# A one-layer hybrid decoder step: gate and rotary arithmetic moved into PSUM, loads and gate parts reordered

## Chip, cores and metric

One core of one Trainium2 chip runs one launch of the kernel. The metric is the device time of that launch in microseconds (us).

## What is computed

One layer with two branches, for a prompt of 1024 tokens and 8 decode sequences of 8 new tokens over 4096 cached tokens each (1088 tokens in all, width 1024, everything float32). The reference, cut:

```python
def hybrid_layer(x, pos, ssm_h0, attend, w):
    xn = rmsnorm(x, w["norm_in"])
    u_s, g_s, cq, ckv_raw, kr_raw, g_a, m_s, m_a = split_in(xn @ w["w_in"])
    y_s, h_last = s5_branch(u_s, ssm_h0, w)      # scan, gelu -> zg, then
    #   zg * sigmoid(zg @ ssm_w_glu + ssm_b_glu)    (the gated unit, "GLU")
    y_s = (y_s * silu(g_s)) @ w["w_br_ssm"]
    cq = rmsnorm(cq, w["mla_q_norm"])                     # 384 wide
    q = einsum('blr,rhd->blhd', cq, w["mla_w_uq"])        # 16 heads, 64 + 32
    q_rope = apply_rope(q[..., 64:], cos, sin)
    q_lat = einsum('blhd,chd->blhc', q[..., :64], w["mla_w_uk"])
    ckv = rmsnorm(ckv_raw, w["mla_kv_norm"])              # 256 wide
    k_rope = apply_rope(kr_raw, cos, sin)
    o_lat = attend(q_lat, q_rope, ckv, k_rope)   # causal over the prompt; decode:
    #   32 pages of 128 rows per sequence, found by page_table, and the own 8
    o = einsum('blhc,chd->blhd', o_lat, w["mla_w_uv"])
    y_a = (o * silu(g_a)) @ w["w_br_attn"]
    merged = sigmoid(m_s) * y_s + sigmoid(m_a) * y_a
    return x + merged @ w["w_out"], ...          # then a final rmsnorm
```

## The kernel before

**Precision and form.** Every product is three matmuls: an operand is split into a rounded high part (a cast on ScalarE, ACT) and the rest (a subtraction on VectorE, DVE, or GpSimd, POOL), and `mm3`/`mm3s` (L141 to L168) multiply high by high, high by low and low by high. `split` (L93 to L102) is the helper: casts stand under L96, subtractions under L102. Activations lie transposed in SBUF, 128 channels by 1088 tokens, which are worked in three pieces of 368, 368 and 352 tokens.

**Gate parts.** A dense product against 128 columns of a weight is a part: a load of 512 KB on SyncE's (SP's) queue (`wraw`), a cast and a subtraction of the weight, 24 matmuls for each of the three token pieces (`mm`), and an end for each token piece: for the gates `g_s` and `g_a`, a tanh on ACT into `gst` (L803) and a DVE operation (L804) that multiplies it with the matmul's bank. Gate parts need only the normalised input, so they serve as filler for TensorE (PE) between stages whose other engines are late. `PLAN` says how many parts lie where.

**Order.** Stages are generators; `woven` interleaves their steps by given weights, and a scheduler puts each engine's instructions in order by recorded priority. Each engine works its own list strictly in that order. `pin` and `behind` tie instructions to others by hand. PSUM's banks are handed out by `bank` in two names, `tr` and `sc`, beside `mm` and `acc`.

**The stages in time** (us from the span's start): the input's norm and transposes to 30; the S5 stages with gate parts to 360; the latents (`stage_latents`, 360 to 465), where `cq` and `ckv` are made by `load_wide`'s 384-wide weights (`wraw` cut in pieces of 128, `wwhi`, `wwlo`), then one `turn` per 128 tokens: norm (`cqn`, L868), transposes on PE (L835). Beside it `cache_ropes` gathers the cached rotary keys (`dkr`) with indirect DMAs from POOL, lays them anew on POOL (`dks`, L1234), transposes them on PE and writes high, high and low parts to `kr_dram`. `cache_rows` (the row indices for these gathers, from the page table) stands just ahead of it. `q_rope` (480 to 518) makes the rotary queries: PE's product into a bank, two copies of swapped halves to `qrot` (ACT), their product with the sine table (POOL L903), the bank times the cosine table into `qr` in SBUF (DVE L904), the sum (L905), the split (`qh`, `ql`). Then the values and other keys and queries, and the prompt's attention (677 to 980), set up by `attn_setup` (transposes of `kst`, splits into the K tiles, the `causal` mask's load) and by `dec_setup` (the new tokens' own rotary keys, `kss` and `krs`). The gated unit (`stage_glu`) and other dense parts are woven with the end of that attention and the decode attention (1130 to 1530; `decode`: per 512 cached rows a gather `ck`, its split into `ch` (ACT) and `cl` (POOL, one operation of 1024), transposes, scores, and products with the values). The dense rest runs to the end.

Of the kernel before, what the change touches and what calls it, by code (L numbers as in the profile page):

```python
# [77 lines left out]
class Body:  # L78
# [51 lines left out]
    def load_wide(self, c0, ncol, raws, outs):  # L130
# [39 lines left out]
    def constants(self):  # L170
# [4 lines left out]
        nc.sync.dma_start(self.ident, a["k_ident"])  # L175
# [4 lines left out]
        self.g_dram = {k: d.tile([D, TOK], F32, name=f"g_{k}") for k in ("gs", "ga", "ms", "ma")}  # L180
        self.gates_done, self.marks, self.first_load, self.x_last, self.banks = {}, [], None, None, 0
# [589 lines left out]
    def s5_states(self, sb, ps):  # L771
# [3 lines left out]
        for r, (c0, n) in enumerate(((0, P), (P, P), (2 * P, NPR))):  # L775
# [9 lines left out]
            nc.sync.dma_start(dst, st[:n])  # L785


    def stage_gates(self, keys, raws, outs, sb, ps, first=0, n=KT, pin=False, goals=None, late=False):
        nc = self.nc
        cols = {"gs": C_GS, "ms": C_MS, "ga": C_GA, "ma": C_MA}  # L790
        for key in keys:
# [21 lines left out]
    def stage_latents(self, lp, cq, outs, sb, ps, between):  # L813
# [71 lines left out]
        yield 4.0  # L885
        turn(*last.pop())


    def q_rope(self, s, qsb, sb, ps, tabs):
# [5 lines left out]
        for t0, m in CHUNKS:  # L895
# [3 lines left out]
            q = sb.tile([P, 368], F32, name="qr", bufs=2)[:, :m]  # L899
            r = sb.tile([P, 368], F32, name="qrot", bufs=2)[:, :m]  # L900
# [3 lines left out]
            nc.vector.tensor_mul(q, b[:, :m], tabs[0][:, t0:t0 + m])  # L904
# [827 lines left out]
    def build(self):  # L1732
# [205 lines left out]
```

## Time and profile before

| | before |
|---|---|
| median of 3 runs | 1761.27 us (1760.45 to 1765.47) |
| the profiled execution | 1759.65 us, its span 1757.8 us |
| PE busy | 1688.1 us (96%) |
| DVE / ACT / POOL busy | 66% / 53% / 34% |
| mean granted clock of PE | 0.987 |

The profile is of one execution. The span runs from its first to its last instruction; 1.85 us of the execution lie outside it. Busy times of the engines overlap. The granted clock is PE's share of its full speed; 0.50 is the lower of its two levels.

### The profile page before, as it was taken

The numbers are of one execution on the slowest core, as the hardware profiler recorded it, in microseconds if no ns is written. First come the engines' busy times: TensorE is split into PE (matmuls) and PEld (weight loads), VectorE is DVE, ScalarE is ACT, GpSimd is POOL, SyncE is SP. The second block draws the span as 40 slices with busy tenths as digits, with TensorE's granted clock in tenths as the row PEclk, the third lists the DMA queues.
The fourth block names the chain that finished last, engine by engine and source line by source line (L and its number), as shares of the span: only waits on it lengthen the run. The fifth ranks groups of instructions, "written<-read, shape, count | busy, mean of one in ns | idle before, by whom it ended". The sixth has DMA issues, their size and how long they took to land.

```text
span 1757.8 us, 31271 instructions
## 1 busy us (share of the span) xinstructions
PE 1688.1 (96%) x10954; PEld 1588.1 (90%) x10954; DVE 1158.4 (66%) x2640; ACT 934.4 (53%) x2226; POOL 592.5 (34%) x622
## 2 busy tenths in 40 slices
PE   6999999989999999999998999999999999999997
PEld 5999999989989998999997898998988999899976
DVE  6768898333374343878888788567656666654496
ACT  5146657722354443767777556456656566631144
POOL 1000000013442204656663555654545445400012
PEclk9999999999999999999999999999999999999999
DMA  8555344544478988665667552575555455384322
GB/s 218 123 144 153 110 120 122 144 139 113 138 222 292 315 299 242 159 167 149 189 162 220 141 158 64 179 251 187 179 172 175 156 170 188 120 303 145 101 85 102
DMA packets 258309, 299.52 MB, mean 170 GB/s; under 512 B 40448, under 2 KB 215272, under 8 KB 251880
## 3 DMA queue, kind: packets, MB, share of 16 engines
q1 hardware_dynamic: 247976, 240.90, 47.7%
q0 software_dynamic: 7872, 48.24, 8.1%
q10 hardware_dynamic: 2304, 8.39, 1.3%
q8 instruction: 87, 1.43, 0.4%
q14 instruction: 70, 0.57, 0.1%
HBM read 201.79 MB, written 95.66 MB: 169 GB/s over the span
## 4 chain that ended last, share of the span: by engine, by line
PE 78%; DMA 8%; DVE 4%; issue 4%; ACT 3%; POOL 2%; SPq 1%; POOLq 0%; ACTq 0%; DVEq 0%
PE mm L159 40%; PE sc L1028 5%; PE sc L159 5%; PE acc L1193 4%; PE tr L1064 3%; PE tr L159 3%; DMA ck<-cache_ckv,pidx 2%; PE acc L1077 2%; PE acc L1078 2%; PE sc L1167 2%; PE sc L1256 1%; PE tr L1256 1%; PE tr L1167 1%; POOL cl L102 1%; DMA wraw<-w_in 1%
## 5 line engine op out<-in xcount | busy, mean ns | idle before, releaser
L159 PE MATMUL mm<-xT,whi 128*128 128x368 f32 (+1 forms) x1920 | 503.9, 336 | 8.7 <-ACT xT L253 4.8
L159 PEld LDWEIGHTS mm<-xT,whi 128*128 128x128 f32 x1920 | 340.9, 190 | 12.6 <-ACT xT L253 5.3
L159 PE MATMUL mm<-xT,wlo 128*128 128x368 f32 (+1 forms) x960 | 320.6, 334 | 0.2 <-DVE wlo L102 0.2
L102 POOL TENSOR_TENSOR cl<-ck,ch 128x1024 fp32r<-128x1024 f32 x64 | 154.2, 2411 | 163.8 <-ACT ch L96 149.4
L159 PEld LDWEIGHTS mm<-xT,wlo 128*128 128x128 f32 x960 | 182.4, 190 | 1.6 <-DVE wlo L102 0.5
L96 ACT CAST pTh<-tr 128x256 fp32r<-128x256 f32 (+1 forms) x248 | 110.8, 449 | 85.9 <-PE tr L1064 67.1
L102 DVE TENSOR_TENSOR pTl<-tr,pTh 128x256 fp32r<-128x256 f32 (+1 forms) x248 | 126.3, 512 | 41.2 <-ACT pTh L96 24.2
L1028 PE MATMUL sc<-K,Q 128*128 128x384 f32 (+5 forms) x576 | 131.5, 345 | 4.0 <-ACT p L1040 4.0
L1045 POOL TENSOR_SCALAR p<-p,sm 128x128 f32<-128x128 f32 (+7 forms) x128 | 96.8, 761 | 109.4 <-DVE sm L1044 48.5
L1040 ACT ACTIVATE p<-sc,sm 128x128 f32<-128x128 f32 (+2 forms) x192 | 110.7, 584 | 22.9 <-DVE sm L1035 12.7
L96 ACT CAST whi<-wraw 128x1024 fp32r<-128x1024 f32 (+1 forms) x76 | 73.3, 966 | 93.1 <-PE mm L159 79.9
L1229 POOL DMA_INDIRECT dkr<-cache_krope,pidx x32 | 33.0, 1032 | 264.2 <-DMA gkv<-mla_kv_norm 256.7
L1064 PE MATMUL tr<-ident,p 128*128 128x128 f32 x576 | 112.1, 274 | 7.6 <-DVE pTl L102 6.7
L159 PE MATMUL mm<-z,whi 128*128 128x368 f32 (+1 forms) x384 | 110.4, 349 | 2.3 <-ACT gst L801 2.3
L1032 DVE TENSOR_REDUCE sm<-sc 128x1 f32<-128x128 f32 (+2 forms) x192 | 104.2, 551 | 9.9 <-PE sc L1028 6.8
L159 PE MATMUL mm<-aT,whi 128*128 128x368 f32 (+1 forms) x384 | 107.6, 337 | 1.6 <-ACT th L1432 1.6
L1028 PEld LDWEIGHTS sc<-K,Q 128*128 128x128 f32 x576 | 98.3, 189 | 11.2 <-ACT p L1040 6.3
L159 PE MATMUL mm<-oT,whi 128*128 128x368 f32 (+1 forms) x384 | 94.2, 327 | 0.2 <-DVE gl L1464 0.2
L102 DVE TENSOR_TENSOR wlo<-wraw,whi 128x1024 fp32r<-128x1024 f32 (+1 forms) x54 | 61.6, 1142 | 39.7 <-ACT whi L96 36.1
L1064 PEld LDWEIGHTS tr<-ident,p 128*128 128x128 f32 x576 | 72.2, 140 | 14.3 <-DVE pTl L102 5.1
L96 ACT CAST ch<-ck 128x1024 fp32r<-128x1024 f32 x64 | 67.3, 1053 | 29.1 <-DMA ck<-cache_ckv,pidx 12.7
L1078 PE MATMUL acc<-pTl,Vt 128*128 128x256 f32 (+1 forms) x224 | 81.6, 364 | 0.1
(534 smaller groups left out, 4390.0 us busy)
## 6 DMA issues: line engine op xcount, KB each, us to landing
wraw<-w_in SPq DMA_DIRECT2D x45, 512.0 KB
krT<-kr_dram SPq DMA_DIRECT2D x64, 192.0 KB
kr_dram<-krx SPq DMA_DIRECT2D x64, 128.0 KB
v_dram<-vt SPq DMA_DIRECT2D x32, 256.0 KB
Q<-qn_dram SPq DMA_DIRECT2D x32, 256.0 KB
K<-kn_dram SPq DMA_DIRECT2D x32, 256.0 KB
Vt<-v_dram SPq DMA_DIRECT2D x8, 1024.0 KB
u_dram<-ust SPq DMA_DIRECT2D x64, 68.0 KB
```

Of the source, the lines that this page charges most:

```text
L96: nc.scalar.copy(hi, src)
L102: return e.tensor_sub(lo, src, hi.bitcast(F32))
L159: i = nc.tensor.matmul(ps, row(s, k)[:, wsl], row(m, k)[(slice(None),) + xsl], start=start and k == j == 0, stop=stop and k == nk - 1 and ...
L1028: self.mark(nc.tensor.matmul(s[:, :w], qq[:, i * P:(i + 1) * P], kk[:, k0:k0 + w], start=j == 0, stop=j == 2), j == 0)
L1032: V.reduce_max(sm[:, x:x + 1], s[:, :w], axis=AX.X)
L1040: nc.scalar.activation(p[:, k0:k0 + w], s[:, :w], AF.Exp, bias=sm[:, 2:3], scale=SCALE, accum_out=sm[:, 3 + x:4 + x])
L1045: nc.gpsimd.tensor_scalar(p[:, :n], p[:, :n], sm[:, 5:6], 0.0, op0=ALU.mult, op1=ALU.add)
L1064: self.mark(nc.tensor.transpose(b[:, x * P:(x + 1) * P], ptl[x][:, k * P:(k + 1) * P], self.ident), x == s0)
L1077: self.mark(nc.tensor.matmul(po[:, o0:], w, th[:, o0:], start=k == 0, stop=False))
L1078: nc.tensor.matmul(po[:, o0:], w, tl[:, o0:], start=False, stop=k == nk - 1)
L1167: i = nc.tensor.matmul(s, x[:, k], y[:, k], start=x is qlh and k == 0, stop=False)
L1193: self.mark(nc.tensor.matmul(o[:, :KV], t[:kp, i * P:(i + 1) * P], pv(i)[x], start=j == 0 and i == 0, stop=j == 2 and i == nt - 1), i == 0)
```

## The change

Seven edits that share a file:

1. `cache_rows` runs behind `stage_x` at the start, not ahead of `cache_ropes`; the loads of `ident` and `norm_in`, and the stores of the S5 states (`sto`), go to ACT's queue.
2. `load_wide` loads its pieces at a higher priority, and `w1`'s casts and subtractions are put behind given gate ends; an unused tile (`gap`) shifts what lies behind it in SBUF.
3. One gate part's first step (`beyond`) is taken ahead of the latents' last `turn`.
4. `cache_ropes` transposes `dkr` itself (no `dks`, no POOL copy) and writes two parts, not three; `dec_keys` gathers `krT` with three loads where there was one.
5. `q_rope` keeps product and sum in the PSUM bank; two gate parts are woven with it instead of one behind one; `own_keys` moves ahead of it out of `dec_setup`.
6. `attn_setup` lays its tiles in another order in SBUF and splits by head, not by half; `PLAN` puts 3 gate parts around the attention's start a little earlier.
7. `stage_glu` applies tanh and the gate in the PSUM bank against `zr`, a row block of z loaded again from DRAM, not against a sum made on POOL (`zz`); `decode` makes `cl` in four POOL operations.

```diff
-PLAN = ((6, MQ, MP - 1), (6, MP - 1, MP - 1), (3, MP + 2, MP + 14), ...
+PLAN = ((6, MQ, MP - 1), (6, MP - 1, MP - 1), (3, MP - 1, MP + 12), ...
...
     def load_wide(self, c0, ncol, raws, outs, behind=None):
...
-            nc.sync.dma_start(raw, self.a["w_in"][:, c0 + s:c0 + s + n].rearrange("(k p) c -> p k c", p=P))
-            self.split(hi[:, :, s:s + n], lo[:, :, s:s + n], raw, "act", "dve")
+            with self.tc.high_priority(offset=UW):
+                nc.sync.dma_start(raw, self.a["w_in"][:, c0 + s:c0 + s + n].rearrange("(k p) c -> p k c", p=P))
+            i = nc.scalar.copy(hi[:, :, s:s + n], raw)
+            j = nc.vector.tensor_sub(lo[:, :, s:s + n], raw, hi[:, :, s:s + n].bitcast(F32))
+            if behind is not None:
+                self.behind(i, behind[0])
+                self.behind(j, behind[1])
...
-        nc.sync.dma_start(self.ident, a["k_ident"])
+        nc.scalar.dma_start(self.ident, a["k_ident"])
...
-            nc.sync.dma_start(dst, st[:n])
+            nc.scalar.dma_start(dst, st[:n])
...
-        w1 = self.load_wide(C_CQ, QL, sb, outs)
+        w1 = self.load_wide(C_CQ, QL, sb, outs, self.gate_ends[-4])
...
         yield 4.0
+        yield next(beyond)
         turn(*last.pop())
...
-            q = sb.tile([P, 368], F32, name="qr", bufs=2)[:, :m]
-            r = sb.tile([P, 368], F32, name="qrot", bufs=2)[:, :m]
+            r = sb.tile([P, 368], F32, name="qrot", bufs=4)[:, :m]
...
-            nc.vector.tensor_mul(q, b[:, :m], tabs[0][:, t0:t0 + m])
+            q = b[:, :m]
+            nc.vector.tensor_mul(q, q, tabs[0][:, t0:t0 + m])
             nc.vector.tensor_add(q, q, r)
...
-        self.KTs = [[kp.tile([P, SEQ], F32R, name=f"K{h}{x}") for x in range(2)] for h in range(2)]
-        self.QTs = [[kp.tile([P, SEQ], F32R, name=f"Q{h}{x}") for x in range(2)] for h in range(2)]
+        for n in ("Q11", "K00", "K01", "causal", "Q00", "Q01", "K10", "K11", "Q10"):
+            t[n] = kp.tile([P, P], F32, name=n) if n == "causal" else kp.tile([P, SEQ], F32R, name=n)
...
-            c = slice(half * 512, half * 512 + 512)
-            for h, rows in ((0, slice(64, 128)), (1, slice(0, 64))):
-                hi, lo = self.KTs[h]
+            banks.append(b)
+        for h, rows in ((0, slice(64, 128)), (1, slice(0, 64))):
+            hi, lo = self.KTs[h]
+            for half, b in enumerate(banks):
...
-            if 0 <= j - 1 < n:
-                ks = kss[j - 1] = sb.tile([P, 2, P], F32, name="dks", bufs=2)
-                nc.gpsimd.tensor_copy(ks.rearrange("p g (r i) -> p g r i", i=4), krs.pop(j - 1).rearrange("p g i r -> p g r i"))
...
-                for y, x in enumerate((hi, hi, lo)):
-                    nc.sync.dma_start(self.kr_dram[j - 2, :, y].rearrange("g p k -> p g k"), x.bitcast(F32))
+                for y, x in enumerate((hi, lo)):
+                    nc.sync.dma_start(self.kr_dram[j - 1, y], x.rearrange("p g k -> p (g k)").bitcast(F32))
...
-        nc.sync.dma_start(krT.bitcast(F32), self.kr_dram[j // 2, j % 2].rearrange("y (r i) k -> (y r) (i k)", i=4))
+        for y in range(3):
+            nc.sync.dma_start(krT[y * NR:(y + 1) * NR].bitcast(F32).rearrange("r (i k) -> r i k", i=4),
+                              self.kr_dram[j // 2, y // 2].rearrange("(i r) (g k) -> g r i k", i=4, g=2)[j % 2])
...
-                self.split(*c, rows(b * 8 + g), "act", "pool")
+                src = rows(b * 8 + g)
+                nc.scalar.copy(c[0], src)
+                for i in range(4):
+                    Gp.tensor_sub(c[1][:, i], src[:, i], c[0][:, i].bitcast(F32))
...
-            nc.gpsimd.tensor_add(zz[:, :m].rearrange("p (c t) -> p c t", t=8), zh.rearrange("p t c -> p c t"),
-                                 zl.rearrange("p t c -> p c t"))
-            nc.vector.scalar_tensor_tensor(g[:, :m], th[:, :m], 1.0, g[:, :m], op0=ALU.add, op1=ALU.mult)
-            nc.vector.tensor_mul(zz[:, :m], zz[:, :m], g[:, :m])
-            nc.sync.dma_start(self.a_dram[rows, sl], zz[:, :m])
+            nc.scalar.activation(b, b, AF.Tanh, scale=0.25, bias=bg[:, j:j + 1])
+            nc.vector.scalar_tensor_tensor(b, b, 1.0, zr[:, :, t0 // 8:(t0 + m) // 8], op0=ALU.add, op1=ALU.mult)
+            g = g[:, :m].rearrange("p (c t) -> p c t", t=8)
+            nc.vector.tensor_mul(g, b.rearrange("p t c -> p c t"), g)
...
+                zrow[j] = sb.tile([P, 8, NCK], F32, name="zr", bufs=1)
+                nc.sync.dma_start(zrow[j], self.z_dram[j * P:(j + 1) * P])
...
-                        yield from self.woven((ropes(), 17), (self.stage_gates(first=6, n=7, **gate), W5))
-                        yield from self.stage_gates(first=7, n=8, pin=True, **gate)
+                        self.own_keys(lp, sb, ps)
+                        yield from self.woven((ropes(), 17), (self.stage_gates(first=6, n=8, **gate), 2 * W5))
```

What this does to the lists of the engines, at three places.

SP's list of transfers between the S5 stages' last stores (`y_dram`) and the latents. L121 is an ordinary part's weight, L137 (L140 in the changed kernel) a piece of `load_wide`'s. Before:

```order
L747 DMA y_dram<-Y 16x8x136 x8
L785 DMA ssm_sample<-sto 128x256 x2
L785 DMA ssm_prompt<-sto 32x256
L1209 DMA sel<-k_sel 8x128
L1211 DMA j_4084<-k_j 128x1
L1213 DMA pt<-page_table 8x32x1
L823 DMA gq<-mla_q_norm 128x384
L824 DMA gkv<-mla_kv_norm 128x256
L826 DMA rt<-k_rope_tok 128x288
L137 DMA wraw<-w_in 128x8x128 x2
L121 DMA wraw<-w_in 128x8x128
L806 DMA g_ga<-gst 128x1088
```

and with the change:

```order
L756 DMA y_dram<-Y 16x8x136 x8
L140 DMA wraw<-w_in 128x8x128 x2
L833 DMA gq<-mla_q_norm 128x384
L834 DMA gkv<-mla_kv_norm 128x256
L838 DMA rt<-k_rope_tok 128x288
L122 DMA wraw<-w_in 128x8x128
L816 DMA g_ga<-gst 128x1088
L140 DMA wraw<-w_in 128x8x128 x3
```

The first two wide pieces stand right behind the last store, ahead of the nine transfers that were before them (six of these have left this place); the third comes behind a gate's store in both.

PE's list at the latents' end: `cqn` 128x128 and 128x64 are the transposes of the last two turns, `mm<-xT` the gate part that follows. Before:

```order
L159 MATMUL mm<-wwhi,xT_7_107 64x288
L835 MATMUL sc<-ident,cqn 128x128 x2
L1239 MATMUL sc<-ident,dks 128x128 x2
L835 MATMUL tr<-ident,cqn 128x64 x2
L159 MATMUL mm<-xT_0_92,whi 128x368
L159 MATMUL mm<-xT_0_93,whi 128x368
```

and with the change, first where the gate part begins and then where it ends:

```order
L166 MATMUL mm<-wwhi,xT_7_107 64x288
L847 MATMUL sc<-ident,cqn 128x128 x2
L1258 MATMUL tr<-ident,dkr 128x128 x2
L166 MATMUL mm<-xT_0_92,whi 128x368
L166 MATMUL mm<-xT_0_93,whi 128x368
```

```order
L166 MATMUL mm<-xT_7_107,whi 128x368
L166 MATMUL mm<-xT_7_106,wlo 128x368
L1258 MATMUL sc<-ident,dkr 128x128 x2
L847 MATMUL tr<-ident,cqn 128x64 x2
L166 MATMUL mm<-xT_0_92,whi 128x368
```

Between the two pieces stand the other matmuls of the same 24, which are now ahead of the last turn's two transposes.

DVE's list at the attention's start: `K` are the key splits, `kss` the own keys, the additions of `causal` the first masks. Before:

```order
L102 TENSOR_TENSOR K_7171<-tr,K_7170 64x512
L102 TENSOR_TENSOR K_7173<-tr,K_7172 64x512
L804 SCALAR_TENSOR_TENSOR gst<-gst,mm 128x368 x2
L1131 CAST kss<-krt 64x32
L1132 COPY kss<-kss 64x32
L1133 COPY kss<-kss 64x32
L1031 TENSOR_TENSOR sc<-sc,causal 128x128 x2
L1134 TENSOR_TENSOR kss<-krt,kss 64x32
L102 TENSOR_TENSOR K_7171<-sc,K_7170 64x512
```

and with the change:

```order
L103 TENSOR_TENSOR K_7104<-sc,K_7103 64x512
L103 TENSOR_TENSOR K_7109<-sc,K_7108 64x512
L813 SCALAR_TENSOR_TENSOR gst<-gst,mm 128x368
L103 TENSOR_TENSOR K_7104<-tr,K_7103 64x512
L1050 TENSOR_TENSOR sc<-sc,causal 128x128 x2
L1051 TENSOR_REDUCE sm<-sc 128x1
L813 SCALAR_TENSOR_TENSOR gst<-gst,mm 128x368
```

`kss` is gone from here, and one K split more stands ahead of the masks; a gate's end now stands behind them.

## Rows read from the trace of the kernel before

**Rows 1.** The page: busy time, share of the span and instructions of each engine.

```profile
PE 1688.1 (96%) x10954; PEld 1588.1 (90%) x10954; DVE 1158.4 (66%) x2640; ACT 934.4 (53%) x2226; POOL 592.5 (34%) x622
```

**Rows 2.** PE's waits in the whole span: waited for, us in total, times, longest.

```profile
PE tr L251 <- DVE xst L199: 8.5, 2, 8.3
PE tr L1064 <- DVE pTl L102: 6.7, 6, 2.1
PE tr L1256 <- DMA ck<-cache_ckv,pidx: 5.7, 4, 2.8
...
PE mm L159 <- DVE gst L804: 3.9, 2, 3.5
PE mm L159 <- ACT wwhi L96: 3.6, 1, 3.6
PE tr L835 <- DVE cqn L868: 3.5, 2, 2.0
...
PE tr L1136 <- DVE kss L1134: 1.8, 1, 1.8
...
PE mm L159 <- DVE wwlo L102: 0.8, 1, 0.8
```

**Rows 3.** Windows: us, busy of PE, PEld, DVE, ACT, POOL, granted clock, DMA.

```profile
373.70:377.10 3.40, 3.14 (x10) 3.14 (x11) 1.78 (x3) 0.26 (x1) 0.00 (x0) 0.50 0.68 191
465.90:469.30 3.40, 3.40 (x13) 3.40 (x12) 0.00 (x0) 0.00 (x0) 1.70 (x2) 0.50 0.44 88
517.10:523.90 6.80, 5.91 (x19) 5.91 (x20) 2.05 (x5) 0.58 (x2) 1.84 (x2) 0.50 0.93 283
687.70:691.10 3.40, 3.40 (x13) 3.27 (x11) 1.75 (x4) 0.97 (x3) 2.98 (x4) 0.50 1.02 296
```

**Rows 4.** SP's queue ahead of the latents: start, us, what.

```profile
349.24 3.02 SPq L785 DMA_DIRECT2D ssm_sample<-sto  x2
...
359.38 1.05 SPq L137 DMA_DIRECT2D wraw<-w_in  x2
```

**Rows 5.** ACT in the same stretch: start, us, what, idle before it and its end.

```profile
371.60 1.04 ACT L96 CAST wwhi<-wraw 128x1024 fp32r<-128x1024 f32 x1 [4.13 <-DMA wraw<-w_in]
```

**Rows 6.** POOL in the latents, by start.

```profile
445.99 0.61 POOL L1234 COPY dks<-dkr 128x256 f32<-128x256 f32 x1 [2.80 <-DMA kr_dram<-dks]
```

**Rows 7.** The rotary queries' stage, one window, columns as in group 3.

```profile
495.00:525.00 30.00, 25.71 (x141) 25.09 (x140) 23.60 (x36) 14.73 (x33) 13.75 (x15) 0.89 0.82 234
```

**Rows 8.** Lines L905 and L904: count, ns least/median/most, first and last start, shapes.

```profile
L905 DVE TENSOR_TENSOR qr<-qr,qrot x12: 512/532/1905, 482.3 to 515.9; 128x368 f32<-128x368 f32 x8, 128x352 f32<-128x352 f32 x4
L904 DVE TENSOR_TENSOR qr<-sc,tab x6: 511/529/542, 481.3 to 511.3; 128x368 f32<-128x368 f32 x4, 128x352 f32<-128x352 f32 x2
```

**Rows 9.** DVE's groups, 478 to 518 and (last two) whole span: busy, mean ns, idle before.

```profile
L102 DVE TENSOR_TENSOR ql<-qr,qh 128x368 fp32r<-128x368 f32 (+1 forms) x12 | 10.8, 902 | 1.1 <-ACT qh L96 0.6
...
L1438 DVE SCALAR_TENSOR_TENSOR gl<-th,gl 128x368 f32<-128x368 f32 (+1 forms) x24 | 23.9, 994 | 9.6 <-ACT th L1432 7.4 <-DMA o_dram<-oT 2.1
L1439 DVE TENSOR_TENSOR zz<-zz,gl 128x368 f32<-128x368 f32 (+1 forms) x24 | 19.9, 829 | 0.5
```

**Rows 10.** DVE at the attention's start.

```profile
684.06 0.50 DVE L1031 TENSOR_TENSOR sc<-sc,causal 128x128 f32<-128x128 f32 x2 [4.43 <-DMA causal<-k_causal]
```

**Rows 11.** POOL's groups in the whole span.

```profile
L102 POOL TENSOR_TENSOR cl<-ck,ch 128x1024 fp32r<-128x1024 f32 x64 | 154.2, 2411 | 163.8 <-ACT ch L96 149.4 <-PE sc L1256 14.2
L1090 POOL TENSOR_TENSOR oT<-oT,og 64x512 f32<-64x512 f32 x32 | 41.5, 1298 | 25.4 <-DVE oT L1083 17.7 <-DMA K<-kn_dram 2.6 <-issue 2.6
L1234 POOL COPY dks<-dkr 128x256 f32<-128x256 f32 x32 | 22.1, 690 | 130.2 <-DMA kr_dram<-dks 103.7 <-DVE wlo L102 7.2 <-DVE qr L904 5.3
```

**Rows 12.** SP's queue at the start.

```profile
0.74 0.40 SPq L175 DMA_DIRECT2D ident<-k_ident  x1
```

**Rows 13.** PE's waits, 676 to 692, and the window of the decode attention.

```profile
PE sc L1028 <- ACT p L1040: 1.8, 1, 1.8
...
1130.00:1540.00 410.00, 398.45 (x2668) 367.64 (x2669) 277.98 (x559) 253.03 (x510) 205.73 (x116) 0.99 0.55 180
```

More of the change, by code (lines that the diff above doesn't have):

```diff
@@ L128, in load_w, with load_wide @@
         return res
-    def load_wide(self, c0, ncol, raws, outs):
+    def load_wide(self, c0, ncol, raws, outs, behind=None):
         nc = self.nc
@@ L981, in attn_setup @@
         nc, a = self.nc, self.a
-        self.causal = kp.tile([P, P], F32, name="causal")
+        t = {}
+        for n in ("Q11", "K00", "K01", "causal", "Q00", "Q01", "K10", "K11", "Q10"):
+            t[n] = kp.tile([P, P], F32, name=n) if n == "causal" else kp.tile([P, SEQ], F32R, name=n)
+        self.causal = t["causal"]
         nc.sync.dma_start(self.causal, a["k_causal"])
-        self.KTs = [[kp.tile([P, SEQ], F32R, name=f"K{h}{x}") for x in range(2)] for h in range(2)]
-        self.QTs = [[kp.tile([P, SEQ], F32R, name=f"Q{h}{x}") for x in range(2)] for h in range(2)]
+        self.KTs, self.QTs = ([[t[f"{n}{h}{x}"] for x in range(2)] for h in range(2)] for n in "KQ")
+        banks = []
         for half in range(2):
@@ L1126, in dec_setup, with own_keys @@
                 nc.sync.dma_start(self.qs[r0:r0 + 16].bitcast(F32), qr[half])
-        kst = sb.tile([NS, P + NR], F32, name="kss", tag="p3", bufs=1)
+    def own_keys(self, lp, sb, ps):
+        nc = self.nc
+        kst = sb.tile([NS, P + NR], F32, name="kss", bufs=1)
         khr = kst[:, P:].bitcast(F32R)
@@ L1136, in dec_setup @@
         nc.tensor.transpose(b[:96, :NS], kst[:, :96], self.ident[:NS, :NS])
[L1137 removed]
+        self.krs = lp.tile([96, NS], F32R, name="krs")
         nc.vector.tensor_copy(self.krs, b[:96, :NS])
@@ L1223, in cache_ropes @@
         nc, a = self.nc, self.a
-        krs, kss = {}, {}
+        krs = {}
         n = DB * 4
-        for j in range(n + 2):
+        for j in range(n + 1):
             if j < n:
@@ L1620, in squares @@
             pt = P if i < 8 else NS
-            y = sb.tile([P, 512], F32, name="osq", bufs=1)
+            y = sb.tile([P, 3, 4, NS], F32, name="osq", tag="oms", bufs=1).rearrange("p a b c -> p (a b c)")[:, 0:512]
             nc.scalar.activation(y[:pt], X[:pt, i, halves[c]], AF.Square, accum_out=ss[:pt, i, c:c + 1])
@@ L1757, in front @@
                         yield from self.stage_x(xT, wr, wo, gsb, self.pool(s3, "xs", 2, side=R), ps)
+                    with ExitStack() as s3:
+                        self.cache_rows(self.pool(s3, "krw", 1, side=R), ps)
                     yield from self.stage_u(wr, wo, gsb, ps, 2, NU)
@@ L1780, in qkv @@
                     outs = self.pool(s2, "wsp2", 1)
+                    more = self.stage_gates(first=5, n=6, pin=True, **gate)
                     yield from self.stage_latents(lp, cq, outs, self.pool(s2, "lsb", 2), ps,
-                                                  self.stage_gates(first=4, n=5, pin=True, **gate))
-                yield from self.stage_gates(first=5, n=6, pin=True, **gate)
+                                                  self.stage_gates(first=4, n=5, pin=True, **gate), more)
+                yield from more
                 with ExitStack() as s2:
```

52 lines of the change are left out of this document (28 added, 24 removed).

## The prediction, made before the changed kernel was run

> **What bounds the kernel now.** The page comes first. TensorE (PE) is busy for 1688.1 us, 96% of the span, and no other engine is above 66% [rows 1]. The change leaves PE's matmul work as it is, so it can only win from the 70 us in which PE stands still and from stretches in which PE works at its lower clock. PE's waits over the whole span say where it stands still [rows 2]: 8.3 us at the start, 3.6 and 0.8 for the wide weights, 3.5 for the latents' norms, 3.5 of 3.9 for a gate's end, 1.8 for the own keys, 6.7 for the attention's low parts, 5.7 for cached rows. No wait is large; the gain is a sum of small ones. The windows of the granted clock add something that this list does not show. [...] PE is the bound there, so work that takes 3.4 us at half speed would take 1.7: each such stretch costs 1.7 us (3.4 for the long one) on top of the wait itself. If the wait goes, I expect the slow stretch behind it to go too.
>
> **The change part by part.** Durations are those of the profiled execution, 1759.65 us, which is 1.62 under the median of the three runs; the sum is made on the first and 1.62 is added at the end.
>
> *Start.* The load of `ident` holds SP's queue for 0.40 us ahead of x's first tiles [rows 12], for which PE waits. On ACT's queue it costs nothing, since ACT has no data yet. The second moved load stands behind x's and counts at most the same for the weights. Gain 0.4 to 0.9; I take 0.5, as the first is sure.
>
> *Wide weights.* SP issues the first two pieces at 359.38 [rows 4]; ACT casts the third of the first set only when it lands, at 371.60, after 4.13 us of idleness [rows 5]. PE waits 4.4 us for the cast and the subtraction, and then works 3.4 us at half clock: 6.1 us. With the change the first two pieces follow the last store directly, without the nine transfers that were ahead of them. The third waits for a buffer that the first frees, so it moves with them. The state stores alone began 10 us ahead of the first piece [rows 4], so a third piece that moves forward by half of this already covers the wait. If the third alone stays late, some 2 us are left to win. Range 2 to 6.1; I take 5.5, nearer to the whole.
>
> *Latents' last turns.* PE waits twice for `cqn`, 3.5 us, the longer 2.0, and then has 3.4 us at half clock [rows 2, 3]. The longer stands in front of the last turn's transposes. Now 24 gate matmuls lie ahead of these transposes. The row at 465.9 counts 13 matmuls in 3.40 us at half clock, so I estimate at least 3.1 us for 24 at full clock, over one and a half times the wait. That gains 2.0 and 1.7. The shorter wait, 1.5 us, has another cause: POOL waits 2.80 us in order for a store before the copy `dks`, and the norm's scale stands behind it on POOL [rows 6]. The copy is removed (32 of them, 22.1 us, 103.7 us of such waiting [rows 11]). But POOL's next gather must now wait until PE has read its buffer, so I count 0.9 of the 1.5. Together 4.6, range 2 to 5.2.
>
> *Rotary queries.* PE waits 3.5 us for a gate's end and then has 6.8 us at half clock, together 6.9. The cause is DVE: in a window of 30 us it is busy for 23.6 [rows 7], and the gate's end stands in its list behind the rotary operations. Some of these are stretched while POOL works. `ql` takes 902 ns in the mean [rows 9] and L905 up to 1905 with a median of 532, whereas L904, which reads a PSUM bank, never goes above 542 [rows 8]. The change moves the operand of L905 and of the split into PSUM, so both should take about 0.53; for `ql` alone that is 12 times 0.37, 4.4 us of DVE time in that stage. Against that, two gate parts lie beside it, whose ends DVE must also make, and the bank is held through the whole chain of operations. I take 5.5 of 6.9; the low end is 2, if DVE stays the bound.
>
> [...]
>
> *Attention's start.* DVE stands idle for 4.43 us until the mask `causal` lands, at 684.06 [rows 10]. The own keys and the second K split are queued behind it, and PE waits 1.8 us for the keys, 1.8 for the first probabilities [rows 13] and has 3.4 us at half clock: 5.3 us. The keys leave this place (they are made 200 us earlier under gate matmuls), and all but one K split stand ahead of the mask. The mask's load still stands behind a load of values on SP's queue. If it lands as late, a gate's end is what then waits behind it, and with it PE's `mm` bank. I take 2.5, about half; ends 0 and 5.3.
>
> *Gated unit.* DVE's two operations of a piece take 994 and 829 ns in the mean [rows 9] beside POOL's sums and would take about 0.53: 24 times 0.76 is 18 us of DVE time. But PE waits for DVE's low parts only 6.7 us there, and part of that comes from other POOL work, which stays. The new loads of `zr` (8 of 0.56 MB, one buffer) can only start when DVE is done with the previous block, and DVE would then wait in order with the softmax behind it; where parts follow one another closely, that costs 1 or 2 us. Range -2 to 6.7; I take 2.5.
>
> *Decode.* `cl` in four operations: from 1298 ns for 512 elements and 2411 for 1024 [rows 11], a line gives 0.745 us for 256 and 2.98 for four, 0.57 more than now per tile. POOL is busy for 206 of 410 us in that window, PE for 398 [rows 13], so the time itself is hidden; but the next gather is issued behind it, and the four waits for `ck` (5.7 us) can grow by 0.57 each. On the other side no DVE operation is held for 2.4 us any more. `krT` has three loads in place of one, issued ahead of their tiles. I take a loss of 1, ends a loss of 3 and a gain of 1.
>
> Everything else (PLAN, `osq`, index loads) I count at nothing: it moves filler and small work under matmuls.
>
> Sum: 0.5 + 5.5 + 4.6 + 5.5 + 2.5 + 2.5 - 1 = 20.1. 1759.65 - 20.1 + 1.62 = 1741. All low ends together give 1.4 (with 0.4 for the start) and 1760, all high ends 32.1 and 1729.
>
> **The rivals.** *Half comes back.* The stages stay tight on DVE, DMA or banks, and the wait moves to the next instruction. For it: the mask is still late, DVE is nearly full beside the rotary queries, and the wide weights' third piece still waits for a buffer. Against it: the last turn's cover is longer than its wait. Taking 2.5 off for the mask, 3.5 for the rotary queries and 3.5 for the weights leaves 10.6 and 1751.
>
> *Nothing is left.* The clock stretches and waits reappear elsewhere, and the new `zr` loads hold DVE in several blocks: about 8 blocks by 1 us, 2 more in decode, from the 10.6 just worked out. That is about 1761. For it speaks only that so many places change at once.
>
> *Slower: the gathers of the decode attention.* If every gather is on the path, `cl`'s 0.57 us is paid in all 64 tiles, 36 us, and the time is 1741 + 35 = 1776, as 1 us of it is in the sum. It decides the sign from some 37 of 64 tiles on (21.1 / 0.57). Four waits for `ck` in the whole span speak against it, as does POOL's half idleness. How far ahead of its tile each of the other 60 gathers lands, I have not worked out; this is why the chance is not smaller.
>
> **How the numbers follow.** The forecast has a chance of 0.58, half of it back 0.22, nothing left 0.11, slower 0.09. About 0.3% (5.3 us) is what a measurement of this kernel can tell from no change. The first two cases are faster than that: 0.80. The third is no change: 0.11. The last is slower: 0.09. For the forecast alone I give 1734 to 1748. The range reaches down to 1733 and up over the second case to 1757, which leaves out the last two and little else, under 2 in 10 with a few of the forecast's own.
>
> **What would show it.** Right: no `wwhi`, `cqn` or `kss` among PE's larger waits; granted clock near 1.0 at 360 to 380, 455 to 475, 495 to 525; the sums in PSUM at 0.51 to 0.54 us each; POOL without L1234 and L1436. Wrong: a wait on `gst` behind the rotary queries or behind `causal`, DVE waiting for `zr`, more waits for `ck` in the decode attention, or new stretches at half clock in places that I have counted at nothing.

## The result and the profile after

The changed kernel takes 1734.47 us (median of 5 runs, 1731.04 to 1737.43) beside 1765.26 for the kernel before (5 runs); the ratio, taken over the runs and not from the two medians, is 0.9835 (95% interval 0.9815 to 0.9856). In a second series beside other kernels it took 1731.67, ratio 0.9823 (0.9795 to 0.9850). The medians differ by 30.8 and 30.6 us, where 20 were forecast. Its profiled execution took 1731.04 us, the shortest of the five, with a span of 1729.1; the profile before is 1759.65 us as in the prediction.

The page after, first the busy times, which answer to [rows 1]:

```profile
PE 1676.6 (97%) x10954; PEld 1577.6 (91%) x10954; DVE 1135.2 (66%) x2640; ACT 932.5 (54%) x2226; POOL 567.8 (33%) x758
```

PE has the same 10954 matmuls. It stands still for 52 us instead of 70, and its busy time is 11.5 us shorter because it works less at half clock (its mean granted clock is 0.996, for 0.987). Its waits in the whole span, in the columns of [rows 2]:

```profile
PE tr L260 <- DVE xst L208: 7.7, 1, 7.7
PE tr L1083 <- DVE pTl L103: 5.4, 8, 2.1
PE tr L1278 <- DMA ck<-cache_ckv,pidx: 2.8, 4, 1.1
...
PE mm L166 <- DVE gst L813: 1.6, 2, 1.0
...
PE mm L166 <- DVE wwlo L142: 0.8, 1, 0.8
```

`wwhi`, `cqn` and `kss` are gone from the list, and the largest wait for a gate's end on DVE fell from 3.5 to 1.0. The windows of the stages (busy of PE, PEld, DVE, ACT, POOL, granted clock, DMA) show full clock everywhere where [rows 3, 7] showed half:

```profile
355.00:375.00 20.00, 18.50 (x106) 17.65 (x105) 7.08 (x10) 5.91 (x9) 0.57 (x1) 1.00 0.79 230
440.00:465.00 25.00, 25.00 (x175) 24.70 (x173) 8.05 (x25) 6.78 (x26) 10.22 (x28) 1.00 0.49 151
490.00:520.00 30.00, 29.93 (x190) 29.61 (x189) 17.31 (x37) 15.69 (x38) 11.34 (x10) 1.00 0.95 287
655.00:690.00 35.00, 31.57 (x188) 29.15 (x187) 21.15 (x59) 17.02 (x49) 15.99 (x23) 1.00 0.79 201
```

Two groups of operations answer to [rows 9] and [rows 11]:

```profile
L1458 DVE SCALAR_TENSOR_TENSOR mm<-mm,zr 128x368 f32<-128x368 f32 (+1 forms) x24 | 12.9, 538 | 10.3 <-ACT mm L1457 5.6 <-DMA zr<-z_dram 4.4
L1460 DVE TENSOR_TENSOR gl<-mm,gl 128x368 f32<-128x368 f32 (+1 forms) x24 | 12.7, 529 | 0.3
...
L1341 POOL TENSOR_TENSOR cl<-ck,ch 128x256 fp32r<-128x256 f32 x256 | 189.4, 773 | 155.3 <-ACT ch L1339 154.9
```

**Where the time came from.** Since the matmuls are the same, two profiles can be compared at equal work: the records of PE's matmuls are put in order of time, each counted with its columns at full clock, and one asks when each kernel has done the same sum. The table gives how much earlier (minus) a kernel passes each point than the kernel before, which passes it at the time on the left, and in brackets the step since the point above. One profile per column; the last is an experiment told below.

| kernel before at, us | changed | changed, second series | `cl` in one piece |
|---|---|---|---|
| 30 | -1.92 (-1.92) | -2.05 (-2.05) | -1.87 (-1.87) |
| 345 | -3.74 (-1.82) | -1.58 (+0.47) | -3.63 (-1.76) |
| 400, wide weights | -8.34 (-4.60) | -6.00 (-4.42) | -8.88 (-5.25) |
| 480, latents' end | -13.23 (-4.89) | -10.88 (-4.88) | -13.76 (-4.88) |
| 545, rotary queries | -20.86 (-7.63) | -18.28 (-7.40) | -20.87 (-7.11) |
| 760, attention's start | -20.64 (+0.22) | -18.28 (0.00) | -20.88 (-0.01) |
| 940 | -18.02 (+2.62) | -15.48 (+2.80) | -17.02 (+3.86) |
| 1160, gated unit | -29.69 (-11.67) | -24.64 (-9.16) | -28.55 (-11.53) |
| 1540, decode | -29.59 (+0.10) | -26.19 (-1.55) | -32.58 (-4.03) |
| 1748 | -27.97 (+1.62) | -25.06 (+1.13) | -31.05 (+1.53) |

The steps of the stages repeat within 2.5 us between the two profiles of the changed kernel, and within 0.3 us from 345 to 940, so single edits can be read from them more finely than from the medians. From 1160 to 1540 they are coarser: in the experiments below that leave the decode attention alone, this step lies between a gain of some 3 us and a loss of 5.

### The profile page after: what moved, and what is told of

The parts are those of the page before. It is cut to its first block, busy times and chain, and to the rows that moved or that the text cites. A ratio compares the mean times of both kernels' runs of the same rounds, so it can differ in the third digit from the quotient of the medians.

```text
span 1729.1 us, 31567 instructions
## 1 busy us (share of the span) xinstructions
PE 1676.6 (97%) x10954; PEld 1577.6 (91%) x10954; DVE 1135.2 (66%) x2640; ACT 932.5 (54%) x2226; POOL 567.8 (33%) x758
## 4 chain that ended last, share of the span: by engine, by line
PE 79%; DMA 9%; DVE 4%; ACT 3%; issue 2%; POOL 1%; SPq 1%; POOLq 0%; ACTq 0%; DVEq 0%
PE mm L166 40%; PE sc L166 5%; PE sc L1047 5%; PE acc L1215 4%; PE tr L1083 3%; PE tr L166 3%; DMA ck<-cache_ckv,pidx 3%; PE acc L1097 2%; PE sc L1189 2%; PE acc L1096 2%; PE sc L1278 1%; PE tr L1278 1%; DMA wraw<-w_in 1%; PE tr L1189 1%; POOL cl L1341 1%
## 5 line engine op out<-in xcount | busy, mean ns | idle before, releaser
L1341 POOL TENSOR_TENSOR cl<-ck,ch 128x256 fp32r<-128x256 f32 x256 | 189.4, 773 | 155.3 <-ACT ch L1339 154.9
L1083 PEld LDWEIGHTS tr<-ident,p 128*128 128x128 f32 x576 | 71.8, 140 | 13.5 <-DVE pTl L103 6.8
```

Source lines behind the costliest of these rows:

```text
L1083: self.mark(nc.tensor.transpose(b[:, x * P:(x + 1) * P], ptl[x][:, k * P:(k + 1) * P], self.ident), x == s0)
L1341: Gp.tensor_sub(c[1][:, i], src[:, i], c[0][:, i].bitcast(F32))
```

## The experiments

All but the last two undo one edit of the changed kernel and leave the others. Times are medians, ratios are to the kernel before in the same series.

**The gated unit's end as before.**

```diff
-            nc.scalar.activation(b, b, AF.Tanh, ...)
-            nc.vector.scalar_tensor_tensor(b, b, 1.0, zr[...], op0=ALU.add, op1=ALU.mult)
+            nc.gpsimd.tensor_add(zz[...], zh..., zl...)
+            nc.vector.scalar_tensor_tensor(g[:, :m], th[:, :m], 1.0, g[:, :m], op0=ALU.add, op1=ALU.mult)
+            nc.vector.tensor_mul(zz[:, :m], zz[:, :m], g[:, :m])
```

> The changed kernel with the gated unit's end as before: sum of z's parts on POOL, tanh to SBUF, both DVE operations on SBUF. Theory (the gated unit gave about 9 us, because POOL's sums stretched DVE's operations): the two DVE operations go back to a mean of about 0.99 and 0.83 us, and the time to about 1743 us (ratio to the kernel before 0.988). Rival (the gain between 940 and 1130 came from the gate parts moved by PLAN and from the order of the attention's start): the stretch comes back on DVE, but the time stays at 1732 to 1737 (0.983).

1743.84 us (7 runs), ratio 0.9922 (0.9897 to 0.9948). DVE's two operations of a piece are stretched again, and between 940 and 1160 the step is +1.85 in place of -11.67 or -9.16:

```profile
L1463 DVE SCALAR_TENSOR_TENSOR gl<-th,gl 128x368 f32<-128x368 f32 (+1 forms) x24 | 25.3, 1053 | 9.8 <-ACT th L1457 9.6
L1464 DVE TENSOR_TENSOR zz<-zz,gl 128x368 f32<-128x368 f32 (+1 forms) x24 | 16.3, 680 | 0.5
```

The theory holds as to the place, with 11.0 to 13.5 us in that stage where 9 were expected; the gate parts that PLAN moved do not make this gain. But POOL's sums are only a small part of what stretches DVE. In the kernel before, 15 of the 48 operations take over 0.6 us. Each of the 15 starts while an operation of POOL is under way and ends 0.37 to 0.40 us after that one has ended, and only in 2 of them is it a sum; in the others it is a subtraction (`wlo`, `cl`) or work of the attention (`oT`, `p`). In the changed kernel 25 of the 48 lie beside an operation of POOL, and the longest takes 0.55 us. One such pair before, and one after:

```profile
994.02 2.39 POOL L102 TENSOR_TENSOR wlo<-wraw,whi 128x1024 fp32r<-128x1024 f32 x1 [0.47 <-ACT whi L96]
994.43 2.36 DVE L1438 SCALAR_TENSOR_TENSOR gl<-th,gl 128x352 f32<-128x352 f32 x1 [0.64 <-ACT th L1432]
...
972.42 2.40 POOL L103 TENSOR_TENSOR wlo<-wraw,whi 128x1024 fp32r<-128x1024 f32 x1 [0.50 <-PE mm L166]
972.87 0.53 DVE L1458 SCALAR_TENSOR_TENSOR mm<-mm,zr 128x352 f32<-128x352 f32 x1
```

**POOL's sums added back, DVE's operands left in PSUM.** The 24 sums are made into a tile that nobody reads.

```diff
+            zz = sb.tile([P, 368], F32, name="zz", tag="zz", bufs=1)
+            nc.gpsimd.tensor_add(zz[...], zh..., zl...)
             nc.scalar.activation(b, b, AF.Tanh, ...)
```

> The changed kernel, with POOL's 24 sums of z made as before beside it, into a tile that nobody reads. Theory A (what counts is that DVE's operations take an operand in PSUM and so aren't stretched by POOL): they stay at 0.53 to 0.56 us beside POOL's 37 us of sums, and the time is within 3 us of the changed kernel, 1733 to 1738. Theory B (what counts is that POOL is free; DVE or POOL's other work is held by the sums whatever the operands): DVE's means go above 0.7 us or other subtractions of DVE take over the stretch, and the time is 1740 to 1745.

1732.75 us (4 runs), ratio 0.9855 (0.9815 to 0.9894):

```profile
L1462 DVE SCALAR_TENSOR_TENSOR mm<-mm,zr 128x368 f32<-128x368 f32 (+1 forms) x24 | 12.9, 538 | 10.8 <-ACT mm L1461 5.5 <-DMA zr<-z_dram 5.0
L1464 DVE TENSOR_TENSOR gl<-mm,gl 128x368 f32<-128x368 f32 (+1 forms) x24 | 12.7, 528 | 0.3
...
L1459 POOL TENSOR_TENSOR zz<-z,z 128x368 f32<-128x368 f32 (+1 forms) x24 | 36.5, 1519 | 2.7 <-DVE sm L1051 2.2
```

POOL works its 36.5 us as in the kernel before, and DVE does not notice: 538 and 528 ns, the same as without. Of the 48 operations 31 lie beside some operation of POOL, 9 of them beside a sum, and the longest takes 0.55 us. Theory A holds. What counts for these two operations is where their operands lie, and not that POOL is free. (DVE here still waits 5.0 us for `zr`; that wait was forecast, but no larger wait of PE goes with it.)

**The rotary sum in SBUF again.**

```diff
-            q = b[:, :m]
-            nc.vector.tensor_mul(q, q, tabs[0][:, t0:t0 + m])
+            q = sb.tile([P, 368], F32, name="qr", bufs=2)[:, :m]
+            nc.vector.tensor_mul(q, b[:, :m], tabs[0][:, t0:t0 + m])
```

> The changed kernel with the rotary queries' product and sum in an SBUF tile (qr, two buffers) as before; the two gate parts beside it, own keys and four buffers of qrot stay. Theory (PSUM operands free DVE there): L905's and ql's operations are stretched again to means above 0.7 us, PE waits 3 to 5 us for a gate's end and falls to the lower clock, time about 1741 (0.987). Rival (the wait went because two gate parts are woven evenly beside the stage): DVE is stretched but PE doesn't wait, time 1733 to 1737.

1737.27 us (4 runs), ratio 0.9883 (0.9838 to 0.9928). `ql` takes 668 ns and L918 (L905 before) 595 in the mean, less than the 0.7 expected. The step from 500 to 545 is -5.06, and -7.67 in the changed kernel: PSUM gives 2.6 us of it in a kernel without the copies `dks`. No wait for a gate's end over 0.3 us comes back. The theory fails in size.

**One gate part beside the rotary queries, one behind.**

```diff
-    ... self.woven((ropes(), 17), (self.stage_gates(first=6, n=8, **gate), 2 * W5))
+    ... self.woven((ropes(), 17), (self.stage_gates(first=6, n=7, **gate), W5))
+    yield from self.stage_gates(first=7, n=8, pin=True, **gate)
```

> The changed kernel with one gate part beside the rotary queries and the other behind them, as before; sums stay in PSUM. With the sums in SBUF only 2.5 of the 7.6 us came back at equal work between 480 and 545 us of the kernel before. Theory (the even weaving of two parts gave the other 5): a loss of 4 to 5 us there, with a wait of PE for a gate's end or for the rotary bank, time about 1738. Rival (either of the two, PSUM or weaving, is enough by itself for most of it): a loss under 2.5 us, time 1733 to 1736.

1735.66 us (6 runs), ratio 0.9846 (0.9821 to 0.9872). The step from 480 to 545 is 1.0 us worse than the changed kernel's. The weaving alone isn't the cause either. (The median lies 4.0 us above the changed kernel's in the same series; the other 3 are not placed.)

**The cached keys' copies as before** (`cache_ropes` and `dec_keys` of the kernel before: copy `dks` on POOL, three parts stored, one load of `krT` a tile).

```diff
+                nc.gpsimd.tensor_copy(ks..., krs.pop(j - 1)...)
...
-        for y in range(3):
-            nc.sync.dma_start(krT[y * NR:(y + 1) * NR]..., self.kr_dram[j // 2, y // 2]...)
+        nc.sync.dma_start(krT.bitcast(F32), self.kr_dram[j // 2, j % 2]...)
```

> The changed kernel with cache_ropes and dec_keys as before: copies dks on POOL, three stores a turn, one load of krT a tile. Theory: POOL's copies hold the norms' scales again, PE waits 1.5 us for the last but one cqn between 440 and 480 us (with the gate part ahead of the last turn the other wait stays away), 2 to 2.5 us at equal work with the clock; krT's loads cost nothing, so 1130 to 1540 stays within 2 us. Time about 1737. Rival (three krT loads of short pieces cost the 3 us that PE loses in the decode attention): 1130 to 1540 is 3 us or more better, time 1731 to 1734.

1744.26 us (6 runs), ratio 0.9899 (0.9873 to 0.9925), 13 us above the changed kernel. The profiled execution is the longest of the six, 1749.6 us, so what follows is too large by some 5 us in all. Between 440 and 480 it loses 2.3 us, as expected, and PE waits there for one `cqn`:

```profile
PE tr L847 <- DVE cqn L880: 2.2, 1, 2.2
```

What was not expected: it loses 5 us in the rotary queries' stage (-2.53 from 500 to 545 for -7.67). POOL's and DVE's groups in that stage show why:

```profile
L915 POOL TENSOR_TENSOR qrot<-qrot,tab 128x368 f32<-128x368 f32 (+1 forms) x12 | 11.5, 964 | 7.0 <-ACT qrot L914 6.9
...
L1256 POOL COPY dks<-dkr 128x256 f32<-128x256 f32 x7 | 4.6, 653 | 22.9 <-DMA kr_dram<-dks 18.2 <-DVE vt L103 4.7
```

```profile
L918 DVE TENSOR_TENSOR sc<-sc,qrot 128x368 f32<-128x368 f32 (+1 forms) x7 | 3.8, 542 | 5.4 <-POOL qrot L915 5.4
...
L918 DVE TENSOR_TENSOR tr<-tr,qrot 128x368 f32<-128x368 f32 (+1 forms) x5 | 2.7, 537 | 4.8 <-POOL qrot L915 4.8
```

Seven copies take only 4.6 us of POOL, but POOL stands still 18.2 us in front of them for the stores that free their buffer. The rotary products (`qrot`) stand behind them in POOL's list, and DVE then waits 10.2 us for these. In this variant the stage's stall is a chain from a store over POOL to DVE to PE, which waits 3.0 us for `ql` and 0.7 for a gate's end from 478 to 520. (In the kernel before it was another, as told below.) The rest lies in the decode attention, where it loses 9.7 us from 1160 to 1540: PE waits 7.1 us for `ck`, 3.7 for the gates' ends `gl` and 3.2 for `dacc` in this profile, and its granted clock from 1130 to 1540 is 0.98, for 1.00 in the second profile of the changed kernel. The rival, that three short `krT` loads cost time, finds no support. Whether one load of `krT` is worse than three I have not settled; the stores of the third part and the order of SP's queue changed with it, and some 5 us of this loss may be this execution's own.

**`load_wide` as before.**

```diff
-            with self.tc.high_priority(offset=UW):
-                nc.sync.dma_start(raw, ...)
-            ...
-                self.behind(i, behind[0])
-                self.behind(j, behind[1])
+            nc.sync.dma_start(raw, ...)
+            self.split(hi[:, :, s:s + n], lo[:, :, s:s + n], raw, "act", "dve")
```

> The changed kernel with load_wide as before: loads at their own priority, casts and subtractions not tied to gate ends. The state stores stay on ACT's queue and the row indices at the start, so SP's queue is empty of the other nine transfers. Theory (the loads' priority gave the gain): PE waits 3 to 4 us for wwhi again and runs at half clock behind it, time about 1740 (0.986). Rival (moving the state stores and index loads off this queue alone was enough): no wait over 1 us, time 1732 to 1737.

1741.36 us (4 runs), ratio 0.9908 (0.9877 to 0.9940). The step from 345 to 400 is +2.16 where the changed kernel has -4.60. But PE's wait there is another than expected:

```profile
PE mm L161 <- DVE gst L808: 6.4, 1, 6.4
```

and ACT's list, by start, shows it:

```profile
359.62 1.04 ACT L97 CAST wwhi<-wraw 128x1024 fp32r<-128x1024 f32 x1 [9.25 <-DMA wraw<-w_in]
360.58 1.04 ACT L97 CAST whi<-wraw 128x1024 fp32r<-128x1024 f32 x1
361.52 0.46 ACT L807 ACTIVATE gst<-mm 128x352 f32<-128x352 f32 x1
```

The wide weight's cast waits 9.25 us for its load, and a gate's end stands behind it in ACT's list, whose bank PE needs. In the changed kernel such an end (353.36) stands ahead of the first wide cast (357.03). This variant undoes the loads' priority and the ties by `behind` together, so it doesn't show which of the two keeps the casts back; that the ties do is my reading of the code. The rival is refuted: with the queue emptied alone, the stage is worse than in the kernel before.

**No gate step ahead of the last turn.**

```diff
-        yield next(beyond)
         turn(*last.pop())
```

> The changed kernel without the one gate step taken ahead of the latents' last turn. Theory: PE waits 2 us for the last cqn and has 3.4 us at half clock, 3.7 us in all, time about 1738 (0.985); the wait of 1.5 us in front of the turn before doesn't come back, since POOL's copy caused it. Rival (the copy caused both waits): PE waits under 1 us there, time 1732 to 1737.

1738.20 us (4 runs), ratio 0.9894 (0.9866 to 0.9923). The shorter wait stays away, the longer returns:

```profile
454.89 0.30 PE L847 MATMUL sc<-ident,cqn 64*128 64x64 f32 x2 [2.56 <-DVE cqn L880]
...
453.00:470.00 17.00, 15.11 (x92) 14.79 (x93) 6.58 (x18) 5.16 (x13) 4.20 (x8) 1.00 0.53 168
```

(a row of PE's list and the window around it). The loss is 2.6 us at equal work, and no stretch at half clock follows. Together with the 2.3 of the copies this is the whole step of -4.9. (The median lies 4 to 6 us above the changed kernel's; the rest of that falls between 1160 and 1540 and has no cause here.)

**`ident` and `norm_in` on SP's queue again.**

```diff
-        nc.scalar.dma_start(self.ident, a["k_ident"])
+        nc.sync.dma_start(self.ident, a["k_ident"])
...
-                nc.scalar.dma_start(nrm, ...)
+                nc.sync.dma_start(nrm, ...)
```

> The changed kernel with the loads of ident and norm_in on SP's queue as before. Theory A (0.4 us of queue time each): PE's first matmul 0.4 to 0.6 us later, the whole within 1 us at equal work, by 60 us from the start 1 us later at most. Theory B (the first weights' earlier landing took away the wait for xT and the half clock behind it, 1.9 us by 30 us and 3.2 by 200): a stretch at half clock near 29 us comes back and the shift at equal work is 2 to 3 us from there on. Time 1735 or 1738; the trace tells more than the time.

1734.34 us (4 runs), ratio 0.9883 (0.9850 to 0.9915). The shift is -1.32 by 30 us and -2.74 by 200, for -1.92 and -3.22: theory A. The queue gives some 0.5 us at most, since other variants that keep the moved loads scatter from -0.92 to -2.08 by 30 us. The other 2.7 are not undone with it: PE's wait for `xT`, made from x's tiles, is 4.8 us in the kernel before, 1.9 in this variant and 1.6 in the changed kernel, whose granted clock from 28 to 33 us is 1.00. The kernel before works at half clock there:

```profile
28.95:32.40 3.45, 2.89 (x12) 2.79 (x12) 3.45 (x11) 2.73 (x6) 0.54 (x1) 0.51 1.04 245
```

The earlier `cache_rows` is left as a cause, and wasn't tried.

**`attn_setup` as before.**

```diff
-        for n in ("Q11", "K00", "K01", "causal", "Q00", "Q01", "K10", "K11", "Q10"):
+        self.causal = kp.tile([P, P], F32, name="causal")
...
-        for h, rows in ((0, slice(64, 128)), (1, slice(0, 64))):
-            for half, b in enumerate(banks):
+            c = slice(half * 512, half * 512 + 512)
+            for h, rows in ((0, slice(64, 128)), (1, slice(0, 64))):
```

> The changed kernel with attn_setup as before (tiles in the old order in SBUF, splits by half). Theory (own keys moved away took the wait, the order of operands only shifts it): PE's loss between 640 and 720 us at equal work is within 2 us of the changed kernel's, time 1732 to 1738. Rival (the new layout lets the K and Q loads start earlier): the first scores come 3 us later, PE stalls 2 to 4 us with half clock behind it, time about 1740.

1730.83 us (4 runs), ratio 0.9861 (0.9830 to 0.9892). The step from 640 to 760 differs from the changed kernel's by 0.2 us: the order of the operands is worth nothing.

**`cl` as one piece**, in two series; in the second beside the changed kernel.

```diff
-                for i in range(4):
-                    Gp.tensor_sub(c[1][:, i], src[:, i], c[0][:, i].bitcast(F32))
+                self.split(*c, rows(b * 8 + g), "act", "pool")
```

> The changed kernel with cl as one POOL operation of 1024 elements as before. Theory (four pieces cost 0.57 us of POOL per tile, which makes later gathers, and at equal work PE loses some 3 us between 1130 and 1540): 1730 to 1732, less waiting for ck. Rival (shorter pieces let DVE in between and so gain): DVE's operations in the decode attention are stretched up to 2 us again, time 1736 to 1740.

> The changed kernel itself, beside the other kernels of this call: 1731 to 1737 us, ratio to the kernel before 0.982 to 0.987.

> The changed kernel with cl in one POOL operation once more, timed beside the changed kernel. Theory (four pieces cost 3 us in the decode attention): 3 us below the changed kernel, 1728 to 1732. Rival (chance between runs): within 1 us of it.

1730.13 us (4 runs, ratio 0.9850, 0.9806 to 0.9894), then 1730.18 (5 runs, 0.9815, 0.9787 to 0.9843) beside 1731.67 for the changed kernel. By time the two are not told apart. At equal work the decode attention is better with one piece in both profiles (-4.03 and -4.24 from 1160 to 1540, for +0.10 and -1.55). Both lie beyond the gain of some 3 us that is the best of the other experiments there; the size of the advantage isn't settled. In the first series' profile no wait for `ck` is among the largest, and `cl` takes 36 us less of POOL:

```profile
L103 POOL TENSOR_TENSOR cl<-ck,ch 128x1024 fp32r<-128x1024 f32 x64 | 153.7, 2402 | 182.6 <-ACT ch L97 182.4
```

It is the fastest version of the study by its medians, but by 1.5 us in the same series, where the changed kernel's two series differ by 2.8.

## Why the prediction was right, and where its terms were not

The direction and the mechanism held: small stalls were removed one by one. The sum was 20, where 25 and 28 us came at equal work in the two profiles and 31 by the medians. So the range held by luck: 1734.47 lies 0.5 us above its lower end, and the 1731.67 of the second series lies below it. Term by term, at equal work:

- *Start*, 0.5 forecast: the queue gave that. Another 2.7 us come with the landing of x's later tiles (a load of `xt` on the chain that ended last lands at 22.46 us instead of 25.87) and a stretch at half clock that I had not counted.
- *Wide weights*, 5.5: 4.6. The first two pieces are now issued at 351.36 instead of 359.38, and PE's waits are 0.8 and 0.7:

```profile
351.36 1.02 SPq L140 DMA_DIRECT2D wraw<-w_in  x2
```

I had credited the order of loads; where the casts stand among the gates' ends was not in my reading.
- *Latents' last turns*, 4.6: 4.9, as 2.6 for the step ahead and 2.3 for the copies. I had put 3.7 and 0.9. The clock did not follow the first; the second was whole, and POOL's wait for PE's transposes, for which I had put it lower, did no harm: POOL waits 3.7 us for them from 430 to 480, and PE for nothing from 440 to 480.
- *Rotary queries*, 5.5: 7.6. Undone one at a time, PSUM gives 2.6, the weaving 1.0 and the copies `dks`, which I had placed in the term before, 5. Each was undone in a kernel that keeps the other edits, and each stalls by a chain of its own. The kernel before has the chain that I read there: a sum stretched to 1.91 us, ACT's cast `qh` that waits for it, a gate's tanh behind that cast, the gate's end on DVE, and PE:

```profile
512.82 1.91 DVE L905 TENSOR_TENSOR qr<-qr,qrot 128x368 f32<-128x368 f32 x1
...
514.75 0.50 ACT L96 CAST qh<-qr 128x368 fp32r<-128x368 f32 x1 [1.77 <-DVE qr L905]
515.16 1.04 ACT L96 CAST whi<-wraw 128x1024 fp32r<-128x1024 f32 x1
516.11 0.45 ACT L803 ACTIVATE gst<-mm 128x352 f32<-128x352 f32 x1
...
517.43 0.51 DVE L804 SCALAR_TENSOR_TENSOR gst<-gst,mm 128x352 f32<-128x352 f32 x1
...
517.99 0.98 PE L159 MATMUL mm<-xT,whi 128*128 128x368 f32 x2 [3.55 <-DVE gst L804]
```

It doesn't have the chain of the copies: POOL waits only once for their stores in this stage, and DVE only 1.6 us for the rotary products. Of the 103.7 us [rows 11], 76.6 lie between 520 and 680.

```profile
509.68 0.65 POOL L1234 COPY dks<-dkr 128x256 f32<-128x256 f32 x1 [1.28 <-DMA kr_dram<-dks]
```

So "the cause is DVE" stands, and what failed is the share given to PSUM: without the copies on POOL, `ql` from SBUF takes 668 ns and not 902. No run puts the sums and the copies back together.
- *Attention's start*, 2.5: nothing. The sentence on the mask was right:

```profile
662.26 0.50 DVE L1050 TENSOR_TENSOR sc<-sc,causal 128x128 f32<-128x128 f32 x2 [3.45 <-DMA causal<-k_causal]
...
663.00 0.53 DVE L813 SCALAR_TENSOR_TENSOR gst<-gst,mm 128x368 f32<-128x368 f32 x1
```

DVE stands 3.45 us for the mask (4.43 before [rows 10]), a gate's end is what now waits behind it, and PE has lost the few us again by 760, in waits of 1.0 for the gate's end and 1.4 for probabilities and some in the softmax behind.
- *Gated unit*, 2.5: 9 to 12. The step that failed is the bound: I had held the gain under PE's 6.7 us of waits for the low parts and left out the other waits and the stretches at half clock in that stage, though the DVE time saved (18 us) was worked out rightly: it came to 18.2. Its source was read wrongly, since POOL's sums hold 2 of the 15 long operations and other work of POOL the rest.
- *Decode*, a loss of 1: from none to a gain of 1.5, within the scatter of that step. If the pieces lose there, as the two profiles with one piece suggest, something else of the change wins about as much. The edits of `cache_ropes` and `dec_keys` are the candidate, by the experiment that undoes them; the cause is not settled. PE's four waits for `ck` did not grow but fell from 5.7 to 2.8 us. The pieces (0.745 us each in the sum, 0.742 by the line through its two rows) measured 0.773. And DVE's operations are still held beside them: a `wlo` beside four pieces takes 3.77 us, where `dql` beside the one piece took 2.40 in the kernel before.
- Not foreseen: 2.6 us lost between 760 and 940, and 2 to 4 in the variants. From 780 to 830 PE stands still for 3.3 us, and in about the same work before (800 to 850) not at all. DVE's operations of the gelu, which lie in the prompt's attention and read SBUF alone, are stretched more than before, by 7.8 us together:

```profile
780.00:830.00 50.00, 46.72 (x297) 43.41 (x296) 40.39 (x117) 34.59 (x107) 29.61 (x44) 1.00 0.63 172
800.00:850.00 50.00, 50.00 (x322) 47.14 (x321) 40.70 (x126) 37.35 (x112) 32.46 (x48) 1.00 0.67 176
...
L1411 DVE SCALAR_TENSOR_TENSOR gy<-gw,gy 128x156 f32<-128x156 f32 (+1 forms) x56 | 24.6, 439 | 0.9 <-ACT gw L1410 0.5
L1436 DVE SCALAR_TENSOR_TENSOR gy<-gw,gy 128x156 f32<-128x156 f32 (+1 forms) x56 | 32.4, 579 | 2.3 <-ACT gw L1435 1.6 <-DMA z_dram<-gy 0.3
```

(The first and last lines are of the changed kernel.) That fits, but no run tests it, and the cause stays open.

An operand in PSUM cost the gated unit's two operations little. The least that they took on SBUF operands, in the kernel before, was 513 and 506 ns. In PSUM they take 538 and 529 in the mean and never more than 550, so at most 25 ns more in the mean (an estimate from these numbers).

## What to carry to other kernels

Where an operation of DVE runs beside a busy POOL, an operand in PSUM is worth a trial: here the pair in the gated unit went from 994 and 829 ns to 538 and 529, 18 us in all, and with POOL's sums added back it stayed at 538 and 528. To find what stretches an operation, look at what runs beside the long ones, and not at the work that is about to be taken away. Before pricing a stall, look through every in-order list on its chain: here copies of 4.6 us in all held POOL for 18.2 us while they waited for stores, and with it what stood behind them. And where a transfer is moved, look where the scheduler puts its consumers: here a cast that waited 9.25 us for its load stood ahead of work that could run.

## What the runs showed of the hardware

Whether PE's clock falls behind a wait of 1.5 to 2.6 us is not fixed by the program. The changed kernel's two profiles have the same wait of 1.5 us at 275 to 277, the longer of two for `Km`:

```profile
PE tr L748 <- ACT Km L728: 2.7, 2, 1.5
...
PE tr L748 <- ACT Km L728: 2.0, 2, 1.5
```

Behind it the first runs at full clock and the second at half. At 1160 the first runs at half clock, behind waits of 1.6 and 1.9 us, and the second at full, behind one of 2.4. The windows of the first profile and then of the second:

```profile
1160.40:1167.20 6.80, 5.89 (x20) 5.08 (x19) 6.80 (x13) 3.96 (x9) 4.70 (x4) 0.50 0.55 162
278.10:284.90 6.80, 5.52 (x39) 5.32 (x40) 5.44 (x9) 5.47 (x14) 0.00 (x0) 1.00 0.73 208
```

```profile
1160.40:1167.20 6.80, 4.98 (x31) 3.86 (x29) 6.80 (x11) 6.80 (x12) 4.20 (x4) 1.00 0.53 185
278.10:284.90 6.80, 6.22 (x27) 5.90 (x26) 3.57 (x7) 3.60 (x13) 0.00 (x0) 0.50 0.55 167
```

The wait of 2.56 us for `cqn` above had no fall behind it, the one of 2.0 in the kernel before had one [rows 2, 3]. So in these profiles a short wait costs its own length and, some of the time, 1.7 or 3.4 us more (an estimate: half of the stretches of 3.4 and 6.8 us). By this estimate one such stretch can set two executions of one kernel that far apart, and a term for the clock in a forecast should be a chance and not a sum.
